# A hybrid decoder layer on one NeuronCore: four steps per recurrence tile on another engine, and five longer waits in the model that sets the order

## The chip, the core and the metric

The kernel runs on one core of one Trainium2 chip. The metric is device time in microseconds (us), the median of several runs of the whole layer: one sequence of 512 tokens, model width 1024, one layer, float32 throughout.

Engines are named as the profile names them: PE is TensorE (matmuls; PEld is its weight load, which overlaps), DVE is VectorE, ACT is ScalarE, POOL is GpSimd, SP is SyncE, whose queue issues nearly all DMAs. Each engine takes its instructions in the order in which they were laid down.

## What is computed

The layer is a half-step feed-forward block (SwiGLU), a mixing block, a second half-step feed-forward block and a final norm. The change lies in the mixing block. There one projection `h @ w_in` feeds two branches and their gates:

```python
proj = h @ w_in[l]
p_rwkv, p_att, p_gate = jnp.split(proj, [RWKV_COLS, RWKV_COLS + ATT_COLS], axis=-1)
y_rwkv = rwkv7_branch(p_rwkv, ...)      # recurrence over 512 tokens, 8 heads of 64
y_att = attention_branch(p_att, ...)    # 8 query heads, 2 key/value heads, window 128
gate_rwkv, gate_att = jnp.split(jax.nn.sigmoid(p_gate), N_BRANCH, axis=-1)
merged = gate_rwkv * (y_rwkv @ w_branch_rwkv[l]) + gate_att * (y_att @ w_branch_attn[l])
x = x + merged @ w_out[l]
```

The recurrence keeps a 64 by 64 state for each head and steps it for each token; after it come a norm over each head, an affine step, a bonus and a gate:

```python
S = S * w_t[:, :, None, :] + sa[..., None] * b_t[:, :, None, :] + v_t[..., None] * k_t[:, :, None, :]
y_t = jnp.einsum('bhij,bhj->bhi', S, r_t)
...
y = (y - mean) * lax.rsqrt(var + GN_EPS)
y = y * ln_w + ln_b
y = (y + bonus) * g
```

## The kernel before

**Tiles.** Features lie on the 128 partitions and tokens along the free dimension. The recurrence is done in 4 tiles (numbered 0 to 3) of two heads each, and inside a tile in 8 chunks of 64 tokens. The attention branch also has 4 tiles (two query heads each). A wide product takes each weight as two parts of reduced width (`wh` and `wl`, made by L196 on ACT and L197 on DVE from a loaded tile `wr`) and each input as two parts (`xh`, `xl`), in three matmuls (L216 to L218) of 128x512 each.

**The mixing stage** runs from about 350 to 720 us. Its work is written as five lanes and a stream. The dense stream (`dense_stream`) is the projection by `w_in`: 34 jobs of 24 matmuls, in the order k, r, v of tile 0, of tile 1, then keys and values, queries and so on, and the 16 gate jobs last. The lanes are `lane_p` (two lanes: for each tile `prep`, then `solve`), `lane_w` (two lanes: `wkv` for each tile) and `lane_a` (attention). They exchange tiles under these names:

- `prep` makes the scaled inputs `AR` and `BK`, then the gram products (PE rows `sm<-AR,BK`, 16 for a tile in two halves of 8), masked by DVE at L899 into `GT`; then transposes of `BK` (L96), and the centred values (rows `sm<-cen,g`), which are copied into the two halves of `UV` by ACT (L917) and DVE (L918); then the bonus `bv` (L924).
- `solve` inverts small triangular blocks on DVE (L941, L943), with three round trips through DRAM on SP's queue; its result is `GI`.
- `wkv` completes the inverse by blocks (PE rows `sm<-YT,GT`, then `sm<-GI,YT`; copies L1027 on ACT, L1037 on DVE, L1038 on ACT), forms two products that are copied at L1057 and L1058 on ACT, multiplies by the inverse (rows `sm<-t,GI`) and copies the result at L1069 (DVE), L1070 and L1071 (ACT). Then come the products with `AR` (26 rows `sm<-GT,AR 64x64`), a chain of six single matmuls over the chunks (rows `sm<-GT,AR 128x64`), each followed by a scaled copy on ACT (L1109), the outputs (rows `sm<-GT,UV` and `sm<-GT`), and the norm: sums over heads (L810, L811, with the split L805 on ACT and L807 on DVE), a reciprocal root (L817, L818), and L1138 to L1142 on DVE, of which L1139 is the affine step.
- `att` makes the scores `S` (copies L1223 on ACT, L1226 on DVE), their maximum (L1231 on DVE), eight exponentials with a sum each (L1239 on ACT), the division (L1245 on DVE), transposes, and the product with the values.

**What sets the order.** `interleave` takes one step of a lane at a time. It counts time by the matmuls it has laid down (`sp.clock`, in ns). A lane that says `yield 1200.0` is ready again when the clock has moved on by `1.15 * 1200 + 200`; a wait of 300 or less is taken as it is. The first lane that is ready goes next; when none is, the dense stream lays down two k-steps (6 matmuls, 1390 on the clock), and for each stretch of lane work the stream gets a share as well (`RATIO`, `LUMP`). So a longer `yield` puts more dense matmuls between two steps of a lane. Under it a scheduling layer with estimates of its own lays the instructions of all engines in order; only matmuls in a `together()` block keep their places among each other. After the lanes come, in program order, the attention half of the output product (8 jobs of 12 matmuls, PE rows `mm<-yas`, with a product at L1309 on DVE each), the split of the four recurrence tiles (L221 on ACT, L222 on DVE, into `xh` and `xl`), and the recurrence half (rows `mm<-xh` again).

## Time and profile before

| | us |
|---|---|
| median of 3 runs | 1146.1 (1145.75 to 1147.96) |
| the profiled execution | 1146.73, its span 1145.0 |
| PE busy | 1110.8 (97%) |
| DVE busy | 867.9 (76%) |
| ACT busy | 588.8 (51%) |
| POOL busy | 224.4 (20%) |

A busy share is an average over the whole layer. A matmul's end is modelled and neighbours overlap, so a busy PE tells only that something stood on it; its idle time is exact where another engine's signal ended it. The profile says for each such gap who ended it. A wait of PE in the middle of the layer is paid in full at the end when PE has work right through to the end, as it has here.

### The profile page before, as it was taken

To read this page: it belongs to the slowest core of one execution; us is meant where nothing else is said; L and a number is where in the kernel's file an instruction comes from. 1 tells how busy PE (TensorE), PEld (TensorE's weight loads), DVE (VectorE), ACT (ScalarE), POOL (GpSimd) and SP (SyncE) were. 2 spreads that over 40 slices of the span, in tenths; PEclk is the share of its full clock that TensorE was granted. 3 is DMA by queue.
4 is the path that set the end of the run, shared out by engine and by line. 5 is a ranking of instruction groups with operands and counts; after the bars stand their busy time and mean duration, and the time that the engine had idled before them with its cause. 6 is when DMAs were issued, how large, how long until landed. Compare 5 with 4: busy or idle time off the path is not lost.

```text
span 1145.0 us, 19776 instructions
## 1 busy us (share of the span) xinstructions
PE 1110.8 (97%) x7892; PEld 963.3 (84%) x7892; DVE 867.9 (76%) x1149; ACT 588.8 (51%) x943; POOL 224.4 (20%) x164
## 2 busy tenths in 40 slices
PE   9899999999999999899989999999999999999997
PEld 7699899978997687678767877778999899989985
DVE  6978579955988479999697635778996489945865
ACT  5744145523555665557553656467554155523554
POOL 5022024402301000000111220012431034202200
PEclk9999999999999999999999999999999999999999
DMA  9234323432226453434325634933334233432221
GB/s 269 64 92 130 92 76 109 129 94 74 70 74 184 138 182 72 107 100 121 91 82 142 167 105 147 268 118 100 95 111 129 74 93 109 132 96 71 75 92 74
DMA packets 223068, 130.12 MB, mean 114 GB/s; under 512 B 37727, under 2 KB 204448, under 8 KB 222976
## 3 DMA queue, kind: packets, MB, share of 16 engines
q1 hardware_dynamic: 221248, 126.79, 38.4%
q10 hardware_dynamic: 1184, 2.04, 0.6%
q8 instruction: 62, 1.02, 0.4%
q0 software_dynamic: 544, 0.04, 0.1%
q14 instruction: 30, 0.25, 0.1%
HBM read 112.96 MB, written 15.61 MB: 112 GB/s over the span
## 4 chain that ended last, share of the span: by engine, by line
PE 72%; DVE 16%; DMA 4%; ACT 4%; issue 2%; SPq 1%; POOL 0%; ACTq 0%; DVEq 0%
PE sm L441 32%; PE mm L216 9%; PE mm L217 8%; PE mm L218 8%; PE sm L218 3%; PE sm L216 3%; PE sm L217 3%; DVE wl L197 3%; PE sm L90 3%; DVE pr L941 2%; DMA g<-gd 1%; ACT wh L196 1%; DMA wr<-in_ffn_w_gate_dram 1%; DVE xt L400 1%; DVE W L943 1%
## 5 line engine op out<-in xcount | busy, mean ns | idle before, releaser
L197 DVE TENSOR_TENSOR wl<-wr,wh 128x1024 fp32r<-128x1024 f32 (+2 forms) x149 | 208.3, 1398 | 80.8 <-ACT wh L196 80.1
L196 ACT CAST wh<-wr 128x1024 fp32r<-128x1024 f32 (+2 forms) x149 | 147.6, 990 | 219.2 <-PE mm L217 99.5
L429 POOL TENSOR_TENSOR wx<-wr,wx 128x1024 f32<-128x1024 f32 x40 | 115.2, 2881 | 386.2 <-DVE wl L197 249.8
L441 PE MATMUL sm<-th,wh 128*128 128x256 f32 x640 | 181.0, 283 | 0.9 <-DVE xt L429 0.9
L197 DVE TENSOR_TENSOR wl<-wx,wh 128x1024 fp32r<-128x1024 f32 x100 | 160.3, 1609 | 27.4 <-ACT wh L196 26.6
L441 PE MATMUL sm<-tl,wh 128*128 128x256 f32 x640 | 180.2, 282 | 0.0
L441 PE MATMUL sm<-th,wl 128*128 128x256 f32 x640 | 180.1, 281 | 0.0
L196 ACT CAST wh<-wx 128x1024 fp32r<-128x1024 f32 x100 | 104.9, 1049 | 132.2 <-PE sm L441 79.7
L441 PE MATMUL sm<-xh,wl 128*128 128x256 f32 x480 | 135.9, 283 | 0.6 <-DVE wl L197 0.6
L441 PE MATMUL sm<-xh,wh 128*128 128x256 f32 x480 | 136.0, 283 | 0.0
L441 PE MATMUL sm<-xl,wh 128*128 128x256 f32 x480 | 135.7, 283 | 0.0
L216 PE MATMUL mm<-xh,wh 128*128 128x512 f32 x320 | 131.1, 410 | 1.2 <-ACT wh L196 0.9
L218 PE MATMUL mm<-xh,wl 128*128 128x512 f32 x320 | 127.6, 399 | 3.2 <-DVE wl L197 2.9
L217 PE MATMUL mm<-xl,wh 128*128 128x512 f32 x320 | 126.5, 395 | 0.0
L441 PEld LDWEIGHTS sm<-th,wh 128*128 128x128 f32 x640 | 120.7, 189 | 2.1 <-issue 1.4
L441 PEld LDWEIGHTS sm<-tl,wh 128*128 128x128 f32 x640 | 120.6, 189 | 0.0
L441 PEld LDWEIGHTS sm<-th,wl 128*128 128x128 f32 x640 | 120.4, 188 | 0.0
L441 PEld LDWEIGHTS sm<-xh,wl 128*128 128x128 f32 x480 | 91.7, 191 | 0.8 <-DVE wl L197 0.8
L441 PEld LDWEIGHTS sm<-xh,wh 128*128 128x128 f32 x480 | 91.7, 191 | 0.5 <-ACT acc L1346 0.2
L441 PEld LDWEIGHTS sm<-xl,wh 128*128 128x128 f32 x480 | 91.7, 191 | 0.5 <-issue 0.2
L218 PEld LDWEIGHTS mm<-xh,wl 128*128 128x128 f32 x320 | 60.5, 189 | 18.4 <-DVE wl L197 3.8
L216 PEld LDWEIGHTS mm<-xh,wh 128*128 128x128 f32 x320 | 60.5, 189 | 16.1 <-issue 2.0
(391 smaller groups left out, 2259.4 us busy)
## 6 DMA issues: line engine op xcount, KB each, us to landing
wr<-in_ffn_w_down_dram SPq DMA_DIRECT2D x38, 512.0 KB, 4.1
wr<-in_w_in_dram SPq DMA_DIRECT2D x34, 512.0 KB, 4.2
wr<-in_ffn_w_gate_dram SPq DMA_DIRECT2D x42, 256.0 KB, 3.0
wr<-in_ffn_w_up_dram SPq DMA_DIRECT2D x42, 256.0 KB, 3.4
wx<-in_ffn_w_gate_dram SPq DMA_DIRECT2D x40, 256.0 KB, 3.0
wx<-in_ffn_w_up_dram SPq DMA_DIRECT2D x40, 256.0 KB, 3.5
gd<-gt SPq DMA_DIRECT2D x16, 256.0 KB, 2.3
g<-gd SPq DMA_DIRECT2D x16, 256.0 KB, 3.3
```

What stands on the lines that cost most here:

```text
L90: self.keep(self.pe.matmul(out, lhsT=lhsT, rhs=rhs, **k))
L196: s.copy(out=hi[:, c], in_=raw[:, c])
L197: v.tensor_tensor(out=lo[:, c], in0=raw[:, c], in1=hi[:, c].bitcast(F32), op=ALU.subtract)
L216: pe.matmul(acc, lhsT=ah, rhs=bh, start=(first and k == 0), stop=False)
L217: pe.matmul(acc, lhsT=ah, rhs=bl, start=False, stop=False)
L218: pe.matmul(acc, lhsT=al, rhs=bh, start=False, stop=(last and k == n - 1))
L400: v.scalar_tensor_tensor(out=t_[:, 1 + i, :], in0=b0, scalar=g1, in1=b1, op0=ALU.mult, op1=ALU.add if i == 2 else ALU.subtract)
L429: e.tensor_tensor(out=o, in0=a, in1=b, op=op)
L441: pe.matmul(acc, lhsT=x_, rhs=y_, start=first and j == 0 and k == 0 and i == 0, stop=last and k == n - 1 and i == 2, skip_group_check=True)
L941: v.tensor_tensor(out=pv_[:, m], in0=a_[:, m].unsqueeze(2).broadcast_to(sh), in1=b_[:, m].rearrange("p u c -> p c u").unsqueeze(1).broadca ...
L943: v.tensor_reduce(out=o, in_=pv_, axis=AX.X, op=ALU.add)
```

## The change

Three kinds of edits:

1. Four steps of each recurrence tile go from DVE to ACT: the copies L918 (64x512, a half of `UV`), L1037 (32x256, a part of `GI`), L1069 (64x512, a half of `UV`) and the affine step L1139 (128x512), which becomes an activation with scale and bias. All but the affine step read PSUM.
2. Five waits in the order's model are longer: before the gram products 1000 becomes 2400; between their two halves 0 becomes 1400; after the first transposes of `wkv` 1800 becomes 2900; after the division in `att` 1600 becomes 2800; and `WSUM`, the wait in each sum over heads, 1200 becomes 1800.
3. Nothing else: no matmul, no DMA and no buffer is added or taken away. L1139 and L1140 become one line, so that lines behind it are one lower afterwards.

```diff
-WSUM = 1200.0
+WSUM = 1800.0
...
         v.tensor_tensor(out=AR[:, :, 1, :], in0=c3(rm), in1=c3(E2), op=ALU.mult)
-        yield 1000.0
+        yield 2400.0
...
                 v.tensor_tensor(out=GT[:, n2:n2 + 2, h, 0:4, :], in0=pg[h],
                                 in1=gmask.unsqueeze(1).broadcast_to([P, 2, 4, C]), op=ALU.mult)
-            yield 0.0
+            yield 1400.0
...
         s.copy(out=UV[HD:P, :, 0, :], in_=c3(pvv)[HD:P])
-        v.tensor_copy(out=UV[0:HD, :, 1, :], in_=c3(pvv)[0:HD])
+        s.copy(out=UV[0:HD, :, 1, :], in_=c3(pvv)[0:HD])
...
         v.transpose(YTv[64:96], GI[64:96, :, 0:32])
-        yield 1800.0
+        yield 2900.0
...
-        v.tensor_copy(out=GI[0:32, :, 32:64], in_=p2v[0:32])
+        s.copy(out=GI[0:32, :, 32:64], in_=p2v[0:32])
...
-        v.tensor_copy(out=UV[HS[0], :, 0, :], in_=pv_[HS[0]])
+        s.copy(out=UV[HS[0], :, 0, :], in_=pv_[HS[0]])
...
-        v.tensor_scalar(out=ysb, in0=ysb, scalar1=hlnw[:, i:i + 1], scalar2=col("ln_b", i),
-                        op0=ALU.mult, op1=ALU.add)
+        s.activation(ysb, ysb, AF.Identity, scale=hlnw[:, i:i + 1], bias=col("ln_b", i))
...
         v.tensor_tensor(out=S, in0=S, in1=dn.unsqueeze(3).broadcast_to([P, 2, NB, P]), op=ALU.mult)
-        yield 1600.0
+        yield 2800.0
```

What this does to the order is shown at three places. Up to the gram products of tile 0 PE's order is the same in both; it is the same again behind the last tile's last sum over heads, and on every engine from the middle of the product with `w_out` on.

**First place: PE at the two halves of tile 0's gram products.** Before:

```order
L216 MATMUL mm<-xh_140,wh 128x512
L90 MATMUL sm<-AR,BK 128x2x64 x9
L217 MATMUL mm<-xl_148,wh 128x512
L218 MATMUL mm<-xh_140,wl 128x512
L216 MATMUL mm<-xh_141,wh 128x512
L217 MATMUL mm<-xl_149,wh 128x512
L218 MATMUL mm<-xh_141,wl 128x512
L216 MATMUL mm<-xh_142,wh 128x512
L217 MATMUL mm<-xl_150,wh 128x512
L218 MATMUL mm<-xh_142,wl 128x512
L90 MATMUL sm<-AR,BK 128x2x64 x7
```

Nine gram matmuls go together here, and the ninth needs a PSUM tile that the first mask gives back. After:

```order
L218 MATMUL mm<-xh_140,wl 128x512
L90 MATMUL sm<-AR,BK 128x2x64 x8
L810 MATMUL sm<-hi,bones 128x512
L811 MATMUL sm<-lo,bones 128x512
L216 MATMUL mm<-xh_141,wh 128x512
L217 MATMUL mm<-xl_149,wh 128x512
L218 MATMUL mm<-xh_141,wl 128x512
L216 MATMUL mm<-xh_142,wh 128x512
L217 MATMUL mm<-xl_150,wh 128x512
L218 MATMUL mm<-xh_142,wl 128x512
L90 MATMUL sm<-AR,BK 128x2x64 x8
```

The ninth gram matmul no longer stands with the first eight: a sum over heads and six dense matmuls now lie between the halves, and two dense matmuls more lie ahead of them. On DVE, the first mask L899 has a 128x1024 weight split (L197) ahead of it, where a 128x512 product of the bonus (L921) stood.

**Second place: ACT in `wkv` of tile 0.** Before (`S` and `sm` are attention's scores and sums, `t` the two products, `YT` and `GI` the inverse):

```order
L1239 ACTIVATE S_4628,sm<-S_4628,sm,rq 128x128 x4
L1241 ACTIVATE sm<-sm,sink 128x4
L630 ACTIVATE g<-pt,omu 128x512
L196 CAST wh<-wr 128x1024
L697 COPY qn<-mm 128x512
L1027 COPY YT<-sm 32x256 x2
L840 ACTIVATE hl<-g 128x8
L848 ACTIVATE g<-g 128x512
L847 ACTIVATE g<-g 128x512
L849 ACTIVATE g<-g 128x512
L1057 COPY t<-sm 128x512
L1058 COPY t<-sm 128x448
```

All exponentials of that attention tile lie ahead of the chain. After, with the copies L1037 and L1069 now on ACT:

```order
L1027 COPY YT<-sm 32x256 x2
L1222 COPY S_5006<-sm 128x256 x2
L1037 COPY GI<-sm 32x8x32
L1038 COPY GI<-sm 32x8x32
L1238 ACTIVATE S_5006,sm<-S_5006,sm,rq 128x128
L1057 COPY t<-sm 128x512
L1058 COPY t<-sm 128x448
L1238 ACTIVATE S_5006,sm<-S_5006,sm,rq 128x128 x3
L1240 ACTIVATE sm<-sm,sink 128x4
L1069 COPY UV<-sm 64x8x64
L1070 COPY UV<-sm 64x8x64
L1238 ACTIVATE S_5006,sm<-S_5006,sm,rq 128x128
```

The copies L1057 and L1058, which the product with the inverse reads, now stand behind the first exponential of an attention tile (L1239 before, L1238 after), and L1069 and L1070 behind the next three. On PE, `wkv` of tile 0 now begins after 346 dense matmuls of the stage, where it began after 299, and the transposes of the first attention tile, which stood in the middle of it, come ahead of it.

**Third place: PE in the chunk chain of `wkv` of the last tile.** Before, six matmuls of the dense stream stand between any two links of the chain:

```order
L90 MATMUL sm<-GT,AR 128x64
L216 MATMUL mm<-xh_141,wh 128x512
L217 MATMUL mm<-xl_149,wh 128x512
L218 MATMUL mm<-xh_141,wl 128x512
L216 MATMUL mm<-xh_142,wh 128x512
L217 MATMUL mm<-xl_150,wh 128x512
L218 MATMUL mm<-xh_142,wl 128x512
L90 MATMUL sm<-GT,AR 128x64
```

That is so at each of the six links. After, the dense stream has run out, and one to two matmuls of the attention half of the output product (`yas`) and some outputs of the tile itself fill in:

```order
L90 MATMUL sm<-GT,AR 128x64
L90 MATMUL sm<-GT 64x64 x3
L218 MATMUL mm<-yas,wl 128x512
L216 MATMUL mm<-yas,wh 128x512
L90 MATMUL sm<-GT,AR 128x64
L90 MATMUL sm<-GT 64x64 x2
L217 MATMUL mm<-yas,wh 128x512
L218 MATMUL mm<-yas,wl 128x512
L90 MATMUL sm<-GT,AR 128x64
L90 MATMUL sm<-GT 64x64 x2
```

Of the 96 `yas` matmuls, 9 lay ahead of the end of this tile's last sum over heads and 87 behind it; now 37 lie ahead of it and 59 behind.

## Rows read from the trace of the kernel before

**Rows 1.** The page: span and instructions, then each engine's busy us, share and instructions.

```profile
span 1145.0 us, 19776 instructions
PE 1110.8 (97%) x7892; PEld 963.3 (84%) x7892; DVE 867.9 (76%) x1149; ACT 588.8 (51%) x943; POOL 224.4 (20%) x164
```

**Rows 2.** Mixing stage in stretches: length, PE, PEld, DVE, ACT, POOL busy, clock, DMA, GB/s.

```profile
432.00:545.00 113.00, 106.81 (x1094) 84.18 (x1092) 106.49 (x215) 69.24 (x150) 3.88 (x11) 1.00 0.41 101
545.00:580.00 35.00, 34.26 (x345) 27.43 (x342) 24.38 (x61) 21.64 (x53) 2.75 (x7) 1.00 0.35 86
580.00:620.00 40.00, 35.12 (x259) 26.83 (x260) 38.08 (x77) 18.66 (x44) 7.56 (x5) 1.00 0.43 115
620.00:660.00 40.00, 40.00 (x427) 32.42 (x427) 21.16 (x29) 22.31 (x38) 7.46 (x6) 0.96 0.60 161
660.00:700.00 40.00, 38.01 (x450) 30.32 (x449) 14.51 (x20) 19.85 (x37) 7.96 (x7) 1.00 0.32 104
700.00:720.00 20.00, 20.00 (x88) 16.06 (x87) 14.81 (x24) 12.04 (x20) 0.00 (x0) 1.00 0.58 174
```

**Rows 3.** Timeline of PE: start, us, line, out<-in, count [idle before, who ended it].

```profile
436.19 1.16 PE L90 MATMUL sm<-AR,BK 64*128 64x128 f32 x14 [0.95 <-DVE GT L899]
...
459.90 1.16 PE L90 MATMUL sm<-AR,BK 64*128 64x128 f32 x14 [1.11 <-DVE GT L899]
...
480.17 0.50 PE L218 MATMUL mm<-xh,wl 128*128 128x512 f32 x1 [1.91 <-DVE wl L197]
494.00 1.09 PE L96 MATMUL sm<-ident,S 128*128 128x128 f32 x8 [1.31 <-DVE S L1245]
...
547.40 1.61 PE L90 MATMUL sm<-GT,AR 64*64 64x64 f32 x48 [0.74 <-DVE S L1226]
...
591.91 1.38 PE L90 MATMUL sm<-AR,BK 64*128 64x128 f32 x18 [1.02 <-DVE BK L880]
595.98 1.16 PE L90 MATMUL sm<-AR,BK 64*128 64x128 f32 x14 [1.33 <-DVE GT L899]
...
618.56 0.69 PE L90 MATMUL sm<-YT,GT 32*32 32x32 f32 x30 [1.25 <-DVE YT L1017]
...
663.77 1.08 PE L90 MATMUL sm<-GI,YT 32*32 32x32 f32 x32 [0.56 <-ACT YT L1027]
...
695.21 0.50 PE L810 MATMUL sm<-hi,bones 128*128 128x512 f32 x1 [0.64 <-ACT hi L805]
```

**Rows 4.** Two stretches of 2 us behind the wait that ends at 618.56.

```profile
620.00:622.00 2.00, 2.00 (x20) 1.16 (x21) 1.93 (x3) 0.04 (x1) 0.00 (x0) 0.50 0.01 4
622.00:624.00 2.00, 2.00 (x85) 1.87 (x80) 0.55 (x2) 0.36 (x1) 0.00 (x0) 0.70 0.17 40
```

**Rows 5.** Groups by line: the moved steps, then their nearest kin on ACT; us, mean ns.

```profile
L918 DVE COPY UV<-sm 64x512 f32<-64x512 f32 x4 | 2.7, 680 | 3.0 <-ACT UV L917 2.9
L1069 DVE COPY UV<-sm 64x512 f32<-64x512 f32 x4 | 2.7, 676 | 0.0
L1139 DVE TENSOR_SCALAR o<-o,hlnw,vec 128x512 f32<-128x512 f32 x4 | 2.2, 541 | 0.0
L1037 DVE COPY GI<-sm 32x256 f32<-32x256 f32 x4 | 1.6, 404 | 0.6 <-PE sm L90 0.5
...
L877 ACT ACTIVATE g<-g,omka,vec 128x512 f32<-128x512 f32 x4 | 3.3, 815 | 0.4 <-DVE t L873 0.4
L1070 ACT COPY UV<-sm 64x512 f32<-64x512 f32 x4 | 2.3, 582 | 2.3 <-DVE UV L1069 2.3
L1038 ACT COPY GI<-sm 32x256 f32<-32x256 f32 x4 | 1.5, 364 | 5.7 <-DVE GI L1037 5.6
```

**Rows 6.** Groups by line: an exponential of the attention tile, and the row maximum ahead of it.

```profile
L1239 ACT ACTIVATE S<-S,sm,rq 128x128 f32<-128x128 f32 x32 | 15.4, 484 | 3.1 <-DVE sm L1234 3.1
```

```profile
L1231 DVE TENSOR_REDUCE sm<-S 128x8 f32<-128x1024 f32 x4 | 4.9, 1216 | 0.0
```

**Rows 7.** Timeline: the last tile's first block product, and its last split.

```profile
660.94 0.69 PE L90 MATMUL sm<-YT,GT 32*32 32x32 f32 x32
...
712.97 0.68 DVE L222 TENSOR_TENSOR xl<-o,xh 128x512 fp32r<-128x512 f32 x1
```

## The prediction

> **What bounds the kernel now.** I read the page first: PE stands busy for 97% of the span [rows 1], so a microsecond comes back only where PE waits, or runs at its lower clock. The matmuls are the same in both kernels. The second view is the mixing stage in stretches. From 432 to 700 PE is idle for 6.2 + 0.7 + 4.9 + 0 + 2.0 = 13.8 us [rows 2], and these stretches differ: in 432 to 545 and in 580 to 620 DVE is busy for 94% and 95% of the time, in 620 to 700 for 45%. So DVE, at 76% over the whole layer, is nearly a second bound there, and is none later. The third view, PE's timeline, tells who ended each wait: of the ten rows shown [rows 3] the eight up to 620 us were ended by DVE (masks L899, scaled inputs L880, a weight split L197, steps of the softmax L1226 and L1245, transposes L1017), seven of them in its two full stretches, and the two behind 660 by ACT. The last view is the clock. Behind the wait of 1.25 that ends at 618.56 the granted clock was 0.50 for 2 us and 0.70 for 2 more [rows 4]: the lower level (1.2 GHz) in part, which costs 2 x 0.5 + 2 x 0.3 = 1.6 us of matmul time. So 13.8 + 1.6 = 15.4 us is all that an edit of this stage can win here.
>
> **The change, part by part. Steps to ACT.** For each tile DVE loses 0.680 + 0.404 + 0.676 + 0.541 = 2.30 us, 9.2 for four [rows 5]. ACT gains 0.582 + 0.364 + 0.582 for the copies, by their twins on the other half of the same tiles, and for the affine step 0.815, by L877, the nearest activation with scale and bias from memory: 2.34, or 9.4 for four [rows 5]. ACT is busy for 61% of 432 to 545 and less later [rows 2], so the sum fits it; what it costs is order, below. Not all of the 9.2 lies where DVE is short. By the order before, DVE does L918 twice, L1037 twice, L1069 and L1139 once inside 432 to 545 (3.4 us), and L918 and L1139 once in 580 to 620 (1.2 us). If every one of these microseconds came off a wait, the steps alone would give 4.6; if DVE used the room for other early work, nothing. I take no value for it by itself, since the waits below are told one by one.
>
> A rule that speaks against one of the four: L1139 took 541 ns on DVE where the other 128x512 passes took 676 to 680 [rows 5], so it is the cheap one there, and on ACT it is bounded by 815. The Trainium skill (Perfetto Trace Analysis, Optimizing Scalar/DVE Operations) says that DVE is faster where one of its performance modes is available, and to move work to ScalarE where DVE is saturated. By the first half the affine step should have stayed: it lengthens the last tile's chain by 0.3 us, and the forecast would be later by that much at most. The row agrees that DVE is the faster place for it; no row shows it on ACT yet.
>
> **Longer waits.** They put more dense matmuls between a lane's steps; a dense matmul is 20 us / 88 = 0.227 us of PE [rows 2]. Place by place:
> - *Tile 0's gram products, 0.95* [rows 3]. The first mask now has a weight split ahead of it on DVE where a 128x512 product stood, about 0.5 more; PE arrives 2 dense matmuls and a sum over heads later, but those lay ahead in any case, so the wait for the second half stays. I take 1.3 (bounds 0 and 2): +0.35.
> - *The weight split at 480 and the division at 494, 1.91 + 1.31* [rows 3]. DVE ran late there because tile 0's block inverse, attention's scores and two jobs' evacuations came at once. `wkv` of tile 0 now begins 47 dense matmuls (10.7 us) later, and attention's division is wanted only behind 60 dense matmuls in a row. I take 0: -3.2.
> - *The rest up to 580* (6.2 - 0.95 - 3.2 = 2.0, and 0.74 at 547) [rows 2, 3]. Tile 1's gram halves have dense work between them now. Of 2.75 I leave 1.0: -1.75.
> - *New, second place of the order.* The copy L1057 stands behind the first exponential. From the last scores to it: score copies and masked copies, four like L1038 (0.36), the maximum 1.22, small steps of 0.5, the exponential 0.48, the copy 0.58 [rows 5, 6], and 0.5 for signals: 4.7. PE has in that time block products (0.7), 30 products like them (1.1), 6 dense matmuls (1.4) and a sum (0.5): 3.7, so it waits about 1. The later copies stand behind three more exponentials: 0.5. I take +1.5; bounds 0 and 3.1 (four exponentials and two copies, none hidden).
> - *Tile 3's products, 580 to 618*: 4.9 less the 1.25 is 3.6 [rows 2, 3]. They keep their pattern (the mask waits for attention's division and a block inverse on DVE), but come 72 dense matmuls later, with 12 between the halves in place of 5. I leave 2.0: -1.6.
> - *The wait at 618.56, 1.25, and the clock behind it, 1.6* [rows 3, 4]. It hung on the load of `GI`, queued on SP behind a gate job's store; by the two orders PE had 30 dense matmuls of cover from the end of that job to the step that needs `GI`, and has 48 now. Both go: -2.85, if no other cluster of waits drops the clock.
> - *The end, 2.0 in 660 to 700* [rows 2]. This is where the bill comes. The last `wkv` starts when the dense stream is out. Its chain took from 660.94 to 713.65, 52.7 us [rows 7], but 99 dense matmuls (22.5 us) stood between its links, so some 30 us is its own. PE now has 105 matmuls of the attention half and of the next product ahead of the place that needs the last split (23.8 us) and about 11 us of the tile's own: 34.8 us of cover for a chain of 30 to 35. I leave the 2.0 as it is: 0. Bounds -2 and the whole rest of the chain, below.
>
> Sum: 0.35 - 3.2 - 1.75 + 1.5 - 1.6 - 2.85 + 0 = -7.55. The profiled execution took 1146.73 (span 1145.0), 0.6 above the median 1146.1; a difference carries over from one to the other: 1139.2 there, **1138.5** from the median. DMAs, HBM bytes and the feed-forward stages have no term, as nothing there is moved.
>
> **Rivals.** *The end is exposed (slower).* If the last tile's chain keeps its 52.7 us for the reason that its links are slow and not that dense work stood between them (ACT's table loads, the loads of `gd` that ACT's sigmoids wait for, POOL's clears behind the gate products), PE idles 52.7 - 34.8 = 17.9 us: 1138.5 - 2.0 + 17.9 = 1154.4. It decides the sign from a chain of about 34.8 + 2 + 7.6 + 2.3 = 46.7 us on. For it: the two sums over heads at the end already waited for ACT and DVE [rows 3]. Against: ACT is at 50% there and DVE at 36% [rows 2], and each of the six links had 6 dense matmuls, 1.4 us, in it, which are gone. *ACT takes DVE's place (no change).* The waits stay as waits for ACT, whose copies stand behind exponentials: all 15.4 us stay, less little: about 1145.5. For it: 1.0 us of such waits exists already, the ends at 663.77 and 695.21 [rows 3]. Against: ACT's 61% at the fullest. *All waits go*: 1146.1 - 15.4 = 1130.7, or some 1132 with the odd one left. For it: nothing else holds PE. Against: two new waits in the order, above. That the edits do nothing to the order is ruled out by the rows of the change.
>
> **How the numbers follow.** The forecast's case (some waits gone, some new ones, the end about covered; 1134 to 1143.5) gets 0.65, all waits gone 0.13, ACT in DVE's place 0.13, the exposed end 0.09. The range goes from 1132.5, inside the case of all waits gone, to 1146.0, with half of the no-change case: it leaves out the slow end and half of each of the two others. A difference of 0.2%, 2.3 us, is about what a measurement of this kernel can tell from none. Faster by more than that is the forecast's case but for its upper edge, and all waits gone: 0.78; within it 0.13; slower 0.09.
>
> **What would show it.** Right: PE idle in 432 to 700 near 7 us in place of 13.8, no wait of 1 us or more at the weight split L197 or at the division; a wait for ACT of about 1 at the product with tile 0's inverse; DVE below 90% in 432 to 545; clock 1.00 through 620 to 630; L918, L1037, L1069 gone from DVE, at 0.36 to 0.58 on ACT, and the affine step there at 0.6 to 0.8. Wrong: PE idle between the last gate job and the recurrence half of the output product by more than 5 us, or waits for ACT spread over all four `wkv`. The forecast falls if the masks' waits stay whole in spite of the matmuls put between, since then DVE's lateness is older than the step that shows it.

## The result, and the profile after

The change makes the kernel slower: 1153.2 us (median of 4 runs, 1151.7 to 1154.4) against 1145.9 (median of 4, 1143.8 to 1148.0), a ratio of 1.0069 with a 95% interval of 1.0050 to 1.0087. That is 7.3 us more, where 7.6 less were forecast; the time lies 7.2 above the top of the range. The profiled execution took 1154.36 (before 1146.73). Its page, in the rows that answer to [rows 1]:

```profile
span 1152.7 us, 19782 instructions
...
PE 1114.0 (97%) x7892; PEld 967.9 (84%) x7892; DVE 869.2 (75%) x1133; ACT 598.9 (52%) x960; POOL 227.2 (20%) x164
```

The page tells nothing of the loss: PE is at 97% as before. The mixing stage in stretches does (the columns of [rows 2]):

```profile
432.00:545.00 113.00, 107.62 (x1078) 86.63 (x1078) 99.86 (x197) 69.66 (x150) 5.24 (x12) 0.98 0.42 104
545.00:580.00 35.00, 34.33 (x330) 27.19 (x330) 26.64 (x63) 24.02 (x57) 4.22 (x4) 1.00 0.30 71
580.00:620.00 40.00, 35.76 (x227) 28.28 (x228) 35.77 (x59) 19.22 (x46) 6.30 (x6) 0.91 0.43 118
620.00:660.00 40.00, 37.12 (x423) 29.61 (x419) 24.60 (x43) 19.31 (x36) 8.55 (x6) 1.00 0.59 154
660.00:700.00 40.00, 35.76 (x462) 29.09 (x461) 13.71 (x18) 24.77 (x41) 6.67 (x6) 0.96 0.39 121
```

PE idles 5.4 + 0.7 + 4.2 + 2.9 + 4.2 = 17.4 us from 432 to 700, where it idled 13.8 before and 7 were forecast. DVE did get room in the first stretch (88%, it was 94%), and PE's idle time fell there by only 0.8. The granted clock, 1.00 in four of the five stretches of [rows 2], is below it in three of them.

PE's waits from 430 to 747 by the line that ended them (engine, tile and line waiting <- what it waited for: us, times, longest) are other ones than those of [rows 3]:

```profile
PE sm L90 <- DVE GT L899: 4.6, 2, 4.0
PE sm L90 <- ACT AR L1071: 4.0, 1, 4.0
PE sm L90 <- ACT GT L1109: 1.6, 1, 1.6
PE sm L90 <- DVE Pc L1253: 1.4, 1, 1.4
PE sm L90 <- DVE AR L1102: 1.2, 1, 1.2
PE mm L216 <- ACT mg L221: 1.2, 1, 1.2
...
PE sm L90 <- DVE YT L1016: 0.9, 1, 0.9
PE sm L90 <- DVE YT L1017: 0.9, 1, 0.9
```

Two waits of 4 us are new: for the masks L899 of tile 3's gram products (ended at 612.48) and for ACT's copy L1071 in the last tile's `wkv` (ended at 692.52). Behind both, and behind the two waits for `YT` at 496, PE runs at its lower clock for a while. Four stretches of 2 us show it (the clock is the third number from the right; 0.50 is 1.2 GHz throughout, 1.00 is 2.4):

```profile
498.00:500.00 2.00, 2.00 (x33) 1.74 (x34) 2.00 (x2) 1.61 (x5) 1.59 (x1) 0.50 0.41 66
...
612.00:614.00 2.00, 1.52 (x13) 1.52 (x14) 2.00 (x3) 0.00 (x0) 0.00 (x0) 0.50 0.15 20
614.00:616.00 2.00, 2.00 (x8) 1.49 (x7) 2.00 (x4) 0.00 (x0) 0.00 (x0) 0.50 0.39 35
...
694.00:696.00 2.00, 2.00 (x40) 1.88 (x38) 0.61 (x3) 0.03 (x1) 0.29 (x1) 0.52 0.39 118
```

**The balance.** Take the stage from its first gram product to the first product with `w_out`. It lasted 431.81 to 740.64 before and 429.55 to 747.11 after:

```profile
431.81:740.64 308.83, 294.01 (x2736) 232.88 (x2737) 235.81 (x448) 175.42 (x356) 32.02 (x35) 0.99 0.47 127
```

```profile
429.55:747.11 317.56, 297.83 (x2736) 237.57 (x2735) 236.55 (x432) 185.56 (x373) 33.39 (x35) 0.98 0.45 121
```

It is 8.7 us longer. PE idles 19.7 us in it where it idled 14.8: +4.9. For the clock I sum 2 x (1 - granted clock) over the stretches of 2 us from 430 to 750: 6.9 us after, 1.7 before: +5.1. Together that is 10.0, 1.3 more than the stage lost; what is left of the stage without the two is that much shorter (291.0 us, it was 292.3), and no run shows why. (The stage begins 2.3 us earlier after, though PE's order ahead of it is the same: at 57 us the execution before had a longer wait, 3.73 us against 2.94, and behind it 1.7 us of lower clock that the one after did not have. That is no part of the change.) **So in these two executions about half of what the stage lost is lower clock, and the forecast had put the clock at zero.** Over all runs the share is somewhat smaller: the mean granted clock was 0.9908 over the four runs of after, and 0.9931 to 0.9940 in five sets of 12 to 23 runs of before. Of the whole span that is 10.6 us against 6.9 to 7.9, so 2.7 to 3.7 of the 7.3 us.

The moved steps did go, at the prices taken for them:

```profile
L1139 ACT ACTIVATE o<-o,vec,hlnw 128x512 f32<-128x512 f32 x4 | 3.3, 817 | 4.0 <-DVE o L1138 3.9
...
L918 ACT COPY UV<-sm 64x512 f32<-64x512 f32 x4 | 2.3, 580 | 0.0
L1069 ACT COPY UV<-sm 64x512 f32<-64x512 f32 x4 | 2.3, 575 | 3.8 <-PE sm L90 3.8
...
L1037 ACT COPY GI<-sm 32x256 f32<-32x256 f32 x4 | 1.4, 362 | 0.4 <-PE sm L90 0.4
```

The affine step costs 0.82 us on ACT where DVE took 0.54 [rows 5], the value that the prediction bounded it by.

**Why L1071 was late.** ACT's timeline ahead of the wait at the end (start, us, line, out<-in, [idle before <- who ended it]):

```profile
686.11 0.58 ACT L1069 COPY UV<-sm 64x512 f32<-64x512 f32 x1 [1.10 <-PE sm L90]
686.70 0.58 ACT L1070 COPY UV<-sm 64x512 f32<-64x512 f32 x1
691.28 0.63 ACT L1307 ACTIVATE g<-g 128x512 f32<-128x512 f32 x1 [4.00 <-DMA g<-gd]
691.93 0.53 ACT L1071 COPY AR<-sm 128x448 f32<-128x448 f32 x1
```

The input of L1071 was ready with that of L1070. But a sigmoid of the attention half stands between the two, and it waits for its load of `gd`, the gates in DRAM. It reads the row of the last gate job, which GpSimd's multiply left at 682.6, SP stored at 682.7 and SP loaded again at 685.8. PE found 1.7 us of output products to do and idled 4.04. ACT stood at such a load before the change too, for 4.63 us, while PE had twelve dense matmuls to do, and PE did not wait:

```profile
678.07 0.63 ACT L1308 ACTIVATE g<-g 128x512 f32<-128x512 f32 x1 [4.63 <-DMA g<-gd]
```

After the change, the two waits in 645 to 656 (1.25 and 1.63) have a sigmoid at a load ahead of them as well.

### The profile page after: what moved, and what is told of

The parts are those of the page before. It is cut to its first block, busy times and chain, and to the rows that moved or that the text cites. A ratio compares the mean times of both kernels' runs of the same rounds, so it can differ in the third digit from the quotient of the medians.

```text
span 1152.7 us, 19782 instructions
## 1 busy us (share of the span) xinstructions
PE 1114.0 (97%) x7892; PEld 967.9 (84%) x7892; DVE 869.2 (75%) x1133; ACT 598.9 (52%) x960; POOL 227.2 (20%) x164
## 3 DMA queue, kind: packets, MB, share of 16 engines
q10 hardware_dynamic: 1184, 2.04, 0.5%
## 4 chain that ended last, share of the span: by engine, by line
PE 72%; DVE 16%; DMA 4%; ACT 4%; issue 3%; SPq 1%; POOL 0%; ACTq 0%; DVEq 0%
PE sm L441 32%; PE mm L216 8%; PE mm L218 8%; PE mm L217 8%; PE sm L90 4%; PE sm L218 3%; PE sm L216 3%; PE sm L217 3%; DVE wl L197 3%; DVE pr L941 2%; DMA g<-gd 1%; ACT wh L196 1%; DVE xt L400 1%; DMA wr<-in_ffn_w_gate_dram 1%; DMA wr<-in_ffn_w_up_dram 1%
## 5 line engine op out<-in xcount | busy, mean ns | idle before, releaser
L197 DVE TENSOR_TENSOR wl<-wr,wh 128x1024 fp32r<-128x1024 f32 (+2 forms) x149 | 212.0, 1424 | 83.4 <-ACT wh L196 79.5
L197 DVE TENSOR_TENSOR wl<-wx,wh 128x1024 fp32r<-128x1024 f32 x100 | 160.5, 1611 | 27.4 <-ACT wh L196 26.6
L216 PEld LDWEIGHTS mm<-xh,wh 128*128 128x128 f32 x320 | 60.8, 190 | 17.4 <-issue 1.9
```

What stands on the lines that cost most here:

```text
L197: v.tensor_tensor(out=lo[:, c], in0=raw[:, c], in1=hi[:, c].bitcast(F32), op=ALU.subtract)
L216: pe.matmul(acc, lhsT=ah, rhs=bh, start=(first and k == 0), stop=False)
```

## The experiments

My first theory: the longer waits start the last `wkv` when the dense stream has run out, and its bare chain, with ACT standing at loads, is the loss. The rival: the four steps on ACT make every tile's chain longer. Each kernel ran beside the kernel before on the same chip, and the ratio is to those runs. The stage, its idle time and what the clock lost are from one profiled execution each, as above; it can lie 3 us off its kernel's median (e2_waits 1155.1, e15_tail_gates_dve 1139.1).

| run | median us | ratio to before (95%) | stage us | PE idle | lost to clock |
|---|---|---|---|---|---|
| before | 1145.9 | 1 | 308.8 | 14.8 | 1.7 |
| after | 1153.2 | 1.0069 (1.0050-1.0087) | 317.6 | 19.7 | 6.9 |
| e1_moves | 1148.0 | 1.0017 (1.0008-1.0026) | 312.1 | 13.4 | 6.8 |
| e2_waits | 1151.7 | 1.0055 (1.0039-1.0072) | 317.4 | 18.7 | 6.8 |
| e3_half | 1154.8 | 1.0080 (1.0063-1.0096) | 318.5 | 17.7 | 10.2 |
| e4_gate_order | 1162.2 | 1.0145 (1.0130-1.0159) | 326.0 | 24.5 | 8.5 |
| e5_tail | 1149.0 | 1.0039 (1.0026-1.0051) | 310.0 | 15.6 | 1.7 |
| e6_loads | 1152.0 | 1.0056 (1.0038-1.0074) | 313.3 | 15.4 | 6.8 |
| e7_moves_loads | 1147.5 | 1.0020 (1.0007-1.0034) | 308.3 | 14.7 | 0.0 |
| e8_before_loads | 1146.0 | 1.0012 (1.0003-1.0020) | 308.8 | 14.8 | 1.7 |
| e9_masks_first | 1149.1 | 1.0027 (1.0015-1.0038) | 312.5 | 16.5 | 3.4 |
| e10_att_wait | 1150.1 | 1.0034 (1.0022-1.0046) | 314.8 | 18.1 | 5.1 |
| e11_outside_chain | 1150.5 | 1.0042 (1.0029-1.0054) | 312.8 | 15.1 | 5.1 |
| e12_inside_chain | 1146.7 | 1.0008 (0.9999-1.0017) | 308.9 | 15.5 | 1.7 |
| e13_no_pool | 1140.2 | 0.9942 (0.9928-0.9957) | 303.1 | 11.3 | 0.0 |
| e14_before_no_pool | 1138.8 | 0.9941 (0.9926-0.9956) | 302.9 | 8.8 | 3.4 |
| e15_tail_gates_dve | 1142.6 | 0.9966 (0.9949-0.9983) | 300.7 | 9.8 | 0.0 |
| e16_before_gates_dve | 1138.7 | 0.9933 (0.9920-0.9947) | 303.4 | 8.8 | 3.4 |
| e17_change_gates_dve | 1141.9 | 0.9967 (0.9952-0.9982) | 303.5 | 9.6 | 3.4 |
| e18_moves_gates_dve | 1143.0 | 0.9972 (0.9960-0.9985) | 306.1 | 11.3 | 3.4 |

Take idle time and lost clock off the stage, and 290 to 294 us are left in all twenty rows. The two columns, then, hold most of what differs, but for some 3 us.

### One half of the change at a time

**e1_moves**: the four steps on ACT, the waits as before.

```diff
-        v.tensor_copy(out=UV[HS[0], :, 0, :], in_=pv_[HS[0]])
+        s.copy(out=UV[HS[0], :, 0, :], in_=pv_[HS[0]])
...
```

> The four steps on ACT alone, with the five waits of the order's model as before. The last tile's wkv begins after 712 of the 796 dense matmuls of the stage, as before, so 84 of them (19.6 us at 0.233) still lie between its links. Theory, the longer waits are the cost, since they start the last wkv when the dense stream is used up: 1141 to 1147 us, the last tile's stretch from its first block product to the end of the attention half as long as before (56.3 us). Rival, the steps on ACT stand behind exponentials and sigmoids there and lengthen every tile's chain: 1151 us or more, with PE waiting for ACT in all four wkv.

**e2_waits**: the five waits, the steps on DVE.

```diff
-            yield 0.0
+            yield 1400.0
...
```

> The five longer waits alone, with the four steps on DVE. PE's order is that of the change: the last wkv begins after all 796 dense matmuls. Theory, the waits are the cost: 1152 to 1156 us, with the wait of 4 us ahead of the last tile's chunk matrices there again, ended by ACT's copy L1072 behind a sigmoid that waits for its load. Rival, the steps on ACT are the cost: at most 1147 us.

The waits alone cost 6.3 us, the moves alone 2.0; together 8.3 for the 7.3 to 7.9 measured. The rival falls as the main cause: without the moved steps the waits bring a wait of 3.32 at the end, ended by the same copy. But e1 missed its number (and e2 by 0.3). In its trace, ACT stands at a cast of `yas` that waits for its load, L1069 and L1070 come behind it, and PE idles 1.98 for L1071; before, L1069 was on DVE and did not have to wait for that cast. The 6.8 us of clock in the table are that one execution's: over its twelve runs the mean granted clock was 0.9929, as before (0.9931).

**e3_half**: the change with the wait between the gram halves back at 0, so that 66 dense matmuls are left for the last `wkv`.

```diff
-            yield 1400.0
+            yield 0.0
```

> The whole change but for one wait: between the halves of the gram products it is 0 again. The last wkv then begins after 730 of the 796 dense matmuls, so 66 of them (15.4 us) are left to stand between its links. Theory, the end of the stage decides: 1142 to 1147 us, most of the 5.6 us that the last tile's stretch lost are back. Rival, what was lost came from the moved steps or from the other four waits: 1151 us or more.

A miss, and the first theory falls in its broad form. The end is covered again (PE idles 1.06 in its last tile's stretch), and the time is no better. The first tile's `wkv` now waits 2.33 for `YT`, and PE runs long at the lower clock behind that:

```profile
490.00:520.00 30.00, 26.94 (x340) 20.48 (x340) 18.51 (x36) 12.87 (x26) 2.60 (x6) 0.72 0.36 90
```

0.28 x 30 = 8.4 us are lost there. Undoing one of the five waits gives another order with other meetings, not the old one.

### The end of the stage

**e4_gate_order**: the change, with gate rows 8 to 15 computed first.

```diff
-        + " ".join([f"g{c}" for c in range(16)])).split()
+        + " ".join([f"g{c % 16}" for c in range(8, 24)])).split()
```

> The changed kernel, with the sixteen gate jobs in another order: rows 8 to 15 of the gates first, then rows 0 to 7. The sigmoids of the attention half, which read rows 8 to 15 back from DRAM, then no longer wait for the last gate job's store; PE's order of work stays, the last wkv still begins after all 796 dense matmuls. Theory in its narrow form, ACT stands in order at a sigmoid whose load is late (690.9 in the profile of after), and the copy L1071 behind it holds PE for 4.04 us and drops the clock: 1146 to 1149 us, no wait of over 1 us at the chunk matrices of the last tile. Rival, the bare chain of the last tile is slow by itself and another link takes the wait over: 1151 to 1154 us.

At the end it does what was expected: the sigmoids of the attention half wait 0.3 us for `gd` in all (those of the recurrence half 8.3), and the last tile's stretch shrinks from 42.4 to 38.6. But the sigmoids, ready early, now stand among the exponentials of the lanes, and each change of table costs ACT 1.28 us: 21 table loads in the stage, 26.9 us, where after has 8. PE waits 3.4, 2.4 and 4.1 us elsewhere. As a test of the end alone it was not clean, so the next one moves three instructions only.

**e5_tail**: the sigmoid of the last gate row, and those of the recurrence half, go behind the last chunk step.

```diff
+            link = s.activation(at(1, n + 1), pz[:, n, :], AF.Copy, scale=q[:, n:n + 1])
...
+            with tc.issue_after(st[3]["link"].ins):
+                s.activation(m2, m2, AF.Sigmoid)
```

> The changed kernel, with ACT's order altered at one place: the sigmoid that reads the last gate job's row back, and the two sigmoids of the recurrence half that stand near it, go behind the last chunk step of the last tile's wkv. In the profile of after the first of them waits for its load until 691.3 and L1071 stands behind it, PE idles 4.04 us, and the granted clock is 0.62 and 0.52 in the 4 us behind. Theory, ACT standing at a load is what makes the bare end dear: the 4.04 us and the 1.7 us of clock go, 1147 to 1149 us. Rival, the chain of the last tile is slow in itself once no dense matmuls lie between its links: the wait turns up at its next link, 1151.5 to 1154 us.

1149.0, 4.2 below after. The stretch from the last tile's first block product to the end of the attention half, in before, after and e5_tail:

```profile
660.94:717.27 56.33, 54.34 (x520) 43.62 (x519) 27.19 (x41) 30.33 (x54) 7.54 (x7) 1.00 0.40 127
```

```profile
679.58:722.01 42.43, 38.19 (x435) 30.35 (x435) 18.48 (x30) 24.12 (x44) 2.24 (x3) 0.96 0.33 101
```

```profile
678.58:715.55 36.97, 36.64 (x436) 29.11 (x435) 18.11 (x29) 23.53 (x44) 2.24 (x3) 1.00 0.39 122
```

5.5 us shorter than in after: 3.9 of idle time, the rest clock. So the bare chain by itself costs nothing (PE idles 0.33 in it, with no dense matmul left); ACT standing at the load did. This is shown, for this part of the loss: e5 is still 3.8 us above the runs of before beside it.

**e6_loads** (all sigmoids of the attention half behind later gate evacuations, and the casts of `yas` on DVE), **e7_moves_loads** and **e8_before_loads** (the same on e1 and on before):

```diff
-        s.activation(m2, m2, AF.Sigmoid)
+        with tc.issue_after((st[3]["link"] if k == KT - 1 else evac[min(10 + k, 15)]).ins):
+            s.activation(m2, m2, AF.Sigmoid)
...
+            v.tensor_copy(out=h_, in_=o)
```

> The changed kernel, with no step on ACT left that waits for a load in the second half of the stage: each sigmoid of the attention half stands behind a later gate job's evacuation (the last one, and those of the recurrence half, behind the last chunk step), and the four casts of yas are on DVE. Theory: besides the 4.04 of the end, tile 2's waits of 1.25 (DVE behind ACT's late weight split) and 1.63 (a chunk step behind a sigmoid) go, 6.9 us in all, and 1.7 of clock: 1144 to 1147 us. Rival, these waits have other causes: 1151 us or more.

> The four moved steps with the old waits (as in e1_moves), and the same edit of ACT's order and of the casts of yas as in e6_loads. In e1_moves ACT stood 2.64 us at a cast of yas that waits for its load, with the copies L1069, L1070 and L1071 of tile 2 behind it, and PE idled 1.98 us. Theory, the moved copies cost only where ACT stands at a load: that wait and the clock behind it (1.9) go, 1143 to 1146 us. Rival, the steps are slower on ACT anyway, since two copies of a tile now run one behind the other: 1147 to 1149 us as in e1_moves.

> The kernel before with the same edit of ACT's order and of the casts of yas. In the profile of before ACT stands at these loads too (7.1 us at the sigmoids), but the copies behind them had twelve dense matmuls of cover, and PE's two waits for ACT there are 0.56 and 0.64. Theory: no change, 1144.5 to 1147 us. Rival, the edit is worth something by itself, whatever the change: 1143 us or less, and then e6 and e7 are to be read against this run.

e6 missed: the wait of 1.63 went, but DVE's 1.45 for tile 2's L1104 stayed, a wait of 1.33 for `YT` came at the end, and the clock took what was won. e7 lost the 1.98 (1.01 for DVE there now) and is hardly faster than e1 (1147.5, 1148.0); e8 is 0.1% slower than before. So apart from the last tile, ACT at loads is not what costs.

### The masks of tile 3

**e9_masks_first**: e5 with attention's last division behind tile 3's first masks on DVE.

```diff
+            with tc.issue_after(masks[3, 0, 1].ins):
+                v.tensor_tensor(out=S, in0=S, in1=dn.unsqueeze(3).broadcast_to([P, 2, NB, P]), op=ALU.mult)
```

> e5_tail, with one step more moved on DVE: the division of attention's last tile (2.30 us there) goes behind the first two masks of tile 3's gram products. In the trace of e5_tail DVE is busy without a break from 589.5 to 617.9, the masks start at 612.60, some 7.7 us after the products that they read, and PE idles 4.02 us for them. Theory, DVE's queue holds the masks and nothing else: they start 2.3 us earlier, the wait falls to 1.5 to 2 us, and the time by as much or, with the clock behind the wait (1.7), by up to 4: 1145 to 1147 us. Rival, the masks wait for something that is no work on DVE, or the division now holds PE at the transposes of attention: 1148 to 1150 us as in e5_tail.

The wait stayed (4.04): a weight split took the division's place ahead of the masks, and there it took 2.30 us, as the division had. Not the step is slow, but the place.

**e10_att_wait**: e5 with the wait behind attention's division back at 1600.

```diff
-        yield 2800.0
+        yield 1600.0
```

> e5_tail with one of the five longer waits undone: after attention's division it is 1600 again. The gram halves of tile 3 then stand behind 576 and 580 dense matmuls and the last transposes of attention's weights behind 646 (598, 610 and 616 in e5_tail), so the masks no longer meet that division on DVE. Theory, the wait of 4 us at tile 3 comes from steps of three lanes that the longer waits bring together on DVE: it is under 1.5 us here, 1145 to 1148 us. Rival, DVE is late by as much wherever the steps stand, and the time stays at 1149 to 1151 us.

The masks' wait went as expected (0.41), but 2.17 for `BK`, 2.08 in the first block product and 2.30 behind a sigmoid took its place.

**e13_no_pool** (e5 without GpSimd's multiply of the gates) and **e14_before_no_pool** (before without it); both leave a part of the computation out, and the gates stay unscaled:

```diff
-            g.tensor_tensor(out=o, in0=o, in1=rs, op=ALU.mult)
```

> e5_tail without GpSimd's multiply L701 of the sixteen gates by the row scale (left out of the computation: the gates are stored unscaled). In e5_tail, e9 and after, the DVE step with two operands in SBUF that runs beside an L701 takes about a microsecond longer (L941 2.01 where its neighbours take 1.05, a 128x1024 step 2.30 where others take 1.21), two of them just ahead of tile 3's masks. Theory, GpSimd slows DVE there: both go back to 1.05 and 1.21, the masks start 2.0 us earlier and the wait of 4.02 falls to about 2; time 1145 to 1148 us. Rival, those steps are slow for another reason: the wait stays at 4, 1148.5 to 1150.5 us.

> The kernel before without the same multiply L701 (the gates are stored unscaled). DVE is full there too in 432 to 545 and 580 to 620, but only the gate jobs from about 555 on have an L701. Theory: the waits for the masks at 591.9 to 598.4 (1.02, 1.33, 0.58) get shorter by 1 to 2 us in all, 1143.5 to 1145.5 us. Rival, no change: 1145 to 1147 us.

The largest effect of all: 8.8 us against e5, and 7.1 against before. DVE ahead of tile 3's masks in e5_tail, GpSimd beside it, and PE's wait:

```profile
604.24 2.01 DVE L941 TENSOR_TENSOR pr<-Y,U 128x512 f32<-128x512 f32 x1
...
609.78 2.30 DVE L1245 TENSOR_TENSOR S<-S,sm 128x1024 f32<-128x1024 f32 x1
612.00 0.67 DVE L943 TENSOR_REDUCE W<-pr 128x32 f32<-128x512 f32 x1
612.60 1.27 DVE L899 TENSOR_TENSOR GT<-sm,gmask 128x512 f32<-128x512 f32 x2
```

```profile
604.05 1.29 POOL L701 TENSOR_TENSOR gt<-gt,rs 128x512 f32<-128x512 f32 x1 [4.93 <-ACT gt L700]
608.95 2.04 POOL L701 TENSOR_TENSOR gt<-gt,rs 128x512 f32<-128x512 f32 x1 [3.61 <-ACT gt L700]
```

```profile
613.33 1.16 PE L90 MATMUL sm<-AR,BK 64*128 64x128 f32 x14 [4.02 <-DVE GT L899]
```

And the same in e13_no_pool, where lines behind the multiply are one lower:

```profile
601.96 1.07 DVE L940 TENSOR_TENSOR pr<-Y,U 128x512 f32<-128x512 f32 x1
...
606.58 1.22 DVE L1244 TENSOR_TENSOR S<-S,sm 128x1024 f32<-128x1024 f32 x1
607.72 0.68 DVE L942 TENSOR_REDUCE W<-pr 128x32 f32<-128x512 f32 x1
608.31 1.28 DVE L898 TENSOR_TENSOR GT<-sm,gmask 128x512 f32<-128x512 f32 x2
```

```profile
609.04 1.16 PE L90 MATMUL sm<-AR,BK 64*128 64x128 f32 x14 [0.88 <-DVE GT L898]
```

Both steps lose their extra microsecond and the wait falls from 4.02 to 0.88. The Trainium skill (SBUF - State Buffer, SBUF: two separate sides) says that DVE and GpSimd share a port pair as a lock: of a DVE step with two inputs in SBUF and a GpSimd step that reads SBUF, the one that starts first has it for its whole length, and the other is blocked. The trace agrees: L941 starts 0.19 us behind an L701 and takes 2.01 us in place of 1.07, and the second L701, which starts behind a DVE step, takes 2.04 in place of 1.29.

The kernel before pays nearly as much for this multiply, though (7.1 of the 8.8). e14 is the cleanest run here: its matmuls stand in the order of before, all of them, and so do DVE's steps up to 646 us. Up to there seven DVE steps of the stage got shorter by more than 0.2 us, each had stood beside an L701, and they got back 5.0 us together. Of the 6.0 us that PE idles less, 1.3 are the wait at 494, which no L701 can explain (the first one comes at 543). And a gate also reaches DRAM earlier without the multiply; no run tests that apart, but e8 makes it unlikely that it is worth much.

What is GpSimd's part in the loss of the change? Here the runs don't agree. About 3.5 of the 7.3 us are ACT at the end (7.3 less the 3.8 of e5). With the end mended and GpSimd out, e13 is 1.4 above e14 by their medians and 0.1 by their ratios to before, and their stages are as long (303.1 and 302.9): by this pair all or most of the 3.8 is DVE's lateness where GpSimd delays it. But with the gates on DVE, which takes GpSimd out as well (below), e15 is 3.9 above e16, as much as e5 is above before, although the wait for tile 3's masks is 0.44 there. So it is shown that GpSimd makes most of that wait, and not shown what share of the loss it has.

### The moved steps apart, and a kernel that beats both

**e11_outside_chain** (L918 and L1139 alone on ACT) and **e12_inside_chain** (L1037 and L1069 alone):

> The kernel before with two of the four moved steps: the copy L918 and the affine step L1139, which lie outside the chain of wkv. No wait changes. Theory, of the 2 us that the four steps lost in e1_moves the copies inside the chain have all, since L1037 and L1069 now run ahead of their twins on ACT where they ran beside them on DVE: this one 1144 to 1146 us. Rival, any of the moves shifts the order and costs the same: 1147 to 1148.5 us.

> The kernel before with the other two moved steps, the copies L1037 and L1069 inside the chain of wkv; PE's order stays that of before. Theory: PE waits for ACT at the products behind L1070 and L1071, 0.5 to 2 us in one or two tiles, 1147 to 1148.5 us. Rival, the copies are covered by the dense matmuls there: 1145 to 1146.5 us.

The other way round: the pair outside the chain costs 4.8 us, the pair inside 0.9, with an interval that reaches no change. In e11's trace PE's idle time is that of before (15.1) and the clock makes the difference (5.1 against 1.7); over its six runs the mean granted clock was 0.9908, beside it before had 0.9932, and that is 2.8 us. e1, with all four steps, costs 2.5 us less than e11 with two of them, and the clock of its runs (0.9929) makes up 2.4 of that. Why the clock fell more in e11 stays open.

**e15_tail_gates_dve** (on e5) and **e16_before_gates_dve** (on before): each gate evacuated by one DVE multiply out of PSUM, with no GpSimd; **e17_change_gates_dve** on the change, **e18_moves_gates_dve** on e1.

```diff
-GEV = 1
+GEV = 0
```

> e5_tail with each gate evacuated by one DVE multiply out of PSUM in place of ACT's copy L700 and GpSimd's multiply L701 (nothing is left out). DVE gains 0.68 us for each of sixteen gates and loses about 1.0 us of delay for each; ACT loses 0.58. Theory as in e13: 1145 to 1148.5 us. Rival, the added DVE steps stand in front of the masks and the splits and take what they give: 1149 to 1152 us.

> The kernel before with the gates evacuated by DVE alone, as in e15. DVE is near full only in 580 to 620 among the stretches that have gates, with three or four of them. Theory: 0.3 us less of DVE for each, 1144 to 1146 us. Rival, an evacuation now waits in DVE's queue behind steps of the lanes, and PE for the PSUM tile it gives back: 1147 to 1150 us.

> The changed kernel, whole, with the gates evacuated by DVE alone as in e16. Theory, the loss has two parts that don't depend on each other, ACT standing at a load at the bare end (4 to 5 us with its clock) and DVE late at tile 3's masks: only the first is left, 1143.5 to 1148 us, 4 to 8 above e16, with the wait ahead of the last tile's chunk matrices there. Rival, without GpSimd beside DVE the whole loss goes: 1138 to 1141 us.

> The four moved steps with the old waits, and the gates evacuated by DVE alone. Theory, DVE still holds PE in 432 to 500 (0.97, 1.11, 0.59 and 1.30 in e16), where three of the moved steps relieve it, but the copies in the chain then wait for ACT, as in e1_moves: no gain over e16, 1138.5 to 1141 us. Rival, with DVE relieved twice its waits go: 1135 to 1138 us.

e16, the kernel before with one constant changed, beats both kernels: 1138.7, 0.67% below before. e14, without any multiply, is no faster (1138.8), so the 0.68 us that DVE gets for each gate cost nothing that can be measured here. By the medians the change loses there too: e17 is 3.2 above e16, and e18 4.3. Their traces don't show where: in the profiled executions the stage takes 303.5 us in e17 and 303.4 in e16, and what e17 has more lies mostly ahead of the stage, where PE's order is the same; the mean granted clock makes up 1.0 us (0.9931 and 0.9940). What the change still costs without GpSimd stays open. In e17 the waits at the end are 1.10 and 1.10 in place of 4.04: the last gate's store goes out 1.4 us behind the last tile's first block product, where it took 3.1 in after. e5's edit has nothing left to win (e15).

The times of e11 and of e13 to e18 all lay outside the ranges given for theory and for rival. In e13 to e16 the cost of GpSimd's multiply had been put at 0 to 4 us, and the medians give 6 to 9.

## Why the prediction was wrong, point by point

- **What bounds the kernel** was read rightly as far as it went: only PE's waits and its clock are to be won. It missed that in 580 to 620 DVE was near full in part because GpSimd held some of its steps (L1142 took 1.40 us at 580.33, 0.69 in e14). In 432 to 545, the other full stretch, before has only one L701, at 543, and GpSimd explains 1.1 us at most.
- **The steps on ACT**: the prices held (0.82 for the affine step, 0.36 to 0.58 for the copies). The comparison that made the affine step "the cheap one" was misread, though: the 676 and 680 of [rows 5] are copies of 64x512 out of PSUM and not passes of 128x512. And L1139 lies at 578.4 and not in 580 to 620, so 0.7 us of the steps lay there, not 1.2; no term was built on that.
- **Tile 0's gram products**, 0.95 to 1.3: 0.84 after. Right.
- **The weight split and the division, -3.2**: these two waits went, as forecast. In their place PE waits for DVE at the next steps of the same work, 1.40 at L1253 and 0.88 + 0.87 at the transposes L1016 and L1017: 3.15. DVE was busy for 6.6 us less in 432 to 545, and PE idled 0.8 less: the late work was asked for elsewhere. The term is about zero in place of -3.2. This is the first step that failed, and the text's own warning fits it: "DVE's lateness is older than the step that shows it".
- **The rest up to 580 and the second place**: 0.63 for L1057 (1.5 taken), and idle time from 432 to 580 of 6.1 us where the terms left 3.8.
- **Tile 3's products, -1.6**: 4.0 us in one wait, and 3.4 of clock from 610 to 618. The 12 dense matmuls between the halves were no cover for masks that came 7 us late behind a solve and a division on DVE.
- **The wait at 618.56 and its clock, -2.85**: both went (620 to 660 has clock 1.00). But "if no other cluster of waits drops the clock" was the condition, and three did: 6.9 us in place of 0. **This is the largest failed step.** The reading of the old wait was wrong as well: the load of `GI` held L1016, but the wait of PE was ended by L1017, 2.4 us behind the landing of its half of `GI` (615.66).

```profile
614.81 0.43 DVE L1016 STREAM_TRANSPOSE YT<-GI 32x256 f32<-32x256 f32 x1 [1.14 <-DMA GI<-gi]
615.18 1.51 DVE L941 TENSOR_TENSOR pr<-V,Y 64x64 f32<-64x64 f32 x2
616.72 0.28 DVE L943 TENSOR_REDUCE Y<-pr 64x32 f32<-64x128 f32 x1
617.03 1.00 DVE L941 TENSOR_TENSOR pr<-Y,U 64x512 f32<-64x512 f32 x1
618.07 0.44 DVE L1017 STREAM_TRANSPOSE YT<-GI 32x256 f32<-32x256 f32 x1
```

  L1017 stood behind another tile's solve in DVE's queue, and the first row of that was 1.1 us longer beside an L701 (1.51 us, 0.39 in e14). In e14, with the same order and no L701, PE does not wait there.
- **The end, 0**: the cover of 34.8 us was enough for the chain, as e5 shows. What failed is that the chain was priced without what stands in ACT's queue: 4.04 of idle time and 1.7 of clock. (Of the 99 dense matmuls taken to lie between its links, the trace has 93 up to the last sum over heads; that changes little.) The rival "the end is exposed" named these very loads but hung its price on the chain's whole length, 17.9 us, of which a third came true; that its 1154.4 lies within 1.2 us of the time is luck.
- Two places had no term: 620 to 660, where PE had no idle time before and has 2.9 now, and the product behind the stage, where a weight split and `mg` L221 hold PE for 1.3 more.
- The chances: slower got 0.09, too little. The working took off each old wait by itself and let new ones appear at one place only, although the order of the whole stage moved.

## What to carry to other kernels

A wait that ends at a full engine is not removed by reordering: price what that engine is asked for next, and look beside its slow steps for a neighbour that holds them up (here a GpSimd multiply of the gates cost 7 us, as much as the whole change moved). When an order is shifted, read what stands in each queue ahead of a chain's steps, loads above all. And give every new wait of a microsecond or more a price in clock as well.

## What the runs showed of the hardware that I had not expected

**The clock falls in some executions and not in others, for the same waits.** e1 and e7 have the same order on PE throughout, and on DVE and ACT up to 627 us. Both wait about 1.3 us for the mask there (ended at 458.36 and 459.95). Some 4 us behind it the clock was, in e1 and then in e7:

```profile
462.00:464.00 2.00, 2.00 (x11) 1.42 (x12) 1.69 (x2) 0.68 (x2) 0.42 (x2) 0.50 0.18 41
```

```profile
464.00:466.00 2.00, 2.00 (x38) 1.58 (x38) 1.84 (x3) 1.84 (x4) 0.42 (x2) 1.00 0.15 27
```

One fall costs 1.7 us or 3.4 in most traces here, up to 8.4. The runs of one kernel spread by it: the eight of e17 go from 1138.5 us (mean granted clock 0.997) to 1146.0 (0.989).

**A DVE step that starts while GpSimd multiplies** took up to 1.1 us longer if both its operands were in SBUF (in e5_tail L941 2.01 in place of 1.05 and L1245 2.30 in place of 1.21; in before the tiny L1197 1.24 in place of 0.16), and no longer if one was in PSUM: the masks L899 of before took 0.68 beside an L701 as elsewhere.
